# A two-branch merge whose second addend arrives by accumulating DMAs begun on GpSimd

## The chip, the core and the metric

The kernel runs on one core of one Trainium2 chip. The time is what the device took for one execution, in microseconds, and the median of several runs is compared. The profile is of one further execution, so sums made from it are made against its own time.

The names of the engines in the profile are PE (TensorE, the matmuls), PEld (its weight loads), DVE (VectorE), ACT (ScalarE), POOL (GpSimd) and SP (SyncE, which here only begins DMAs). A "q" behind a name is the engine's instruction queue.

## The reference

One step of a decoder layer, in float32, over 1024 prompt rows and 64 sample rows with 1024 channels. The change touches only the merge of its two branches.

```python
h = rmsnorm(x, norm_mix)
q, k, v, gu, gv, ga, gb = split_in(h @ w_in)
o = attention(q, k, v)                        # sliding window of 128, sinks
s = spatial_gating(gelu(gu), layernorm(gelu(gv)))
merged = sigmoid(ga) * (o @ w_pa) + sigmoid(gb) * (s @ w_pb)
x = x + merged @ w_out
x = x + conv_ffn(rmsnorm(x, norm_ffn))        # up, causal conv, gelu gate, down
y = rmsnorm(x, norm_final)
```

## The kernel before, in words

Everything is kept transposed: 128 channels on the partitions, rows along the free dimension. The 1024 channels are eight column blocks, numbered c = 0 to 7. The 1088 rows are cut in two groups: group 0 has 576 rows (the 64 sample rows and half the prompt), group 1 has 512. Each float32 operand of a matmul is split into a high and a low part (ACT casts the high one, DVE subtracts to get the low one), and three matmuls stand for one product; this pair of steps is the helper `split`, lines 40 and 41. For weights the tiles are called wraw, wh and wl, for the merged operand mh and ml.

The stages around the change, in order of time:

- Attention of group 0, mixed with the gMLP branch product (`branch`). For each c and both groups, DVE multiplies the product in PSUM by the gate (line 1072), and SP stores the result to memory, in `mbd[g][c]`.
- Attention of group 1, mixed with the attention branch product of group 0 (`merge(0, c, keep)`). For each c DVE multiplies by the other gate (line 1100, tile stg, 576 wide), and `keep` stores the result to memory, in `msd[c]`.
- The merge of group 1 (`merge(1, c, ...)`): 48 matmuls for each c, then DVE multiplies by the gate (line 1100, 512 wide), adds the gMLP half, which SP had loaded from `mbd[1][c]` into a second staging tile (line 1102), and splits the sum. Beside it, for each c, `hold` loads `msd[c]` and `mbd[0][c]` of group 0 into the tiles m and b, DVE adds them (line 1403), and `operand(0)` splits the sum.
- w_out, first of group 0 and then of group 1 (line 240 again, and the residual add on line 1419), and after it the up projection.

During the last two stages ACT and DVE also prepare the first up-projection weights (`pair_load`, `pair_unit`; tiles ra, rb, s and hl), which are stored to `upd`.

Names that the prediction uses: stg is the staging tile, of which there are four (gates, products and, before, the second addend); mm is the accumulator in PSUM, of which there are two; sg0d is the gate in memory; mask c is the causal mask that POOL applies in attention (line 1277), and s the scores, into which POOL copies a sink column (line 1240).

The program order is written in Python; a scheduler then lays out each engine's instructions in a fixed order, and each engine runs its own in that order and waits on semaphores. A DMA is an instruction in the queue of the engine that begins it, and what stands behind it waits while it waits.

Of the kernel before, what the change touches and what calls it, by code (L numbers as in the profile page):

```python
# [6 lines left out]
F32 = mybir.dt.float32  # L7
# [3 lines left out]
ALU = mybir.AluOpType  # L11
# [4 lines left out]
P = 128  # L16
D = 1024
KD = 8
# [16 lines left out]
def layer(tc, a):  # L35
    nc = tc.nc
    V, S, G, PE = nc.vector, nc.scalar, nc.gpsimd, nc.tensor

    def split(hi, lo, src):
        S.copy(hi, src)  # L40
        V.tensor_sub(lo, src, hi.bitcast(F32))  # L41
# [5 lines left out]
    with ExitStack() as top:  # L47
# [185 lines left out]
        def mm3(ps, chunks, w, hs, k0, k1, nk, clear=True):  # L233

            wh, wl = w
            for lo, c0, c1 in chunks:
                for k in range(k0, k1):
                    ah, al = hs[k]
                    for i, (u, v) in enumerate(((wh, ah), (wh, al), (wl, ah))):
                        PE.matmul(ps[:, lo:lo + c1 - c0], u[:, k, :], v[:, c0:c1],  # L240
                                  start=(clear and k == 0 and i == 0),
                                  stop=(k == nk - 1 and i == 2), skip_group_check=True)
# [91 lines left out]
        dr = lambda name, shape, dt=F32: dram.tile(shape, dt, name=name)  # L334
# [9 lines left out]
        gvd = {name: dr(f"gvd{name}", [P, GW]) for gr in groups for name, _ in gr["toks"]}  # L344
        vnd = [dr(f"vnd{gr['g']}", [P, NG, len(gr["toks"]), P]) for gr in groups]
        sd_ = [[dr(f"sd{g}{c}", [P, 2, n]) for c in range(NG)] for g, n in ((0, 576), (1, 512))]
        msd = [dr(f"msd{c}", [P, 576]) for c in range(KD)]
        upd = [[dr(f"upd{f}_{j}", [P, 2, 4, P]) for j in range(7)] for f in range(NPRE)]
        mbd = [[dr(f"mbd{g}{c}", [P, n]) for c in range(KD)] for g, n in ((0, 576), (1, 512))]

# [7 lines left out]
        with ExitStack() as ph1:  # L358
# [9 lines left out]
            def stage(n):  # L368
                return stg.tile([P, 576], F32, name="stg")[:, :n]
# [346 lines left out]
            none = lambda: None  # L716
# [319 lines left out]
            def acc2():  # L1036
                return pmm.tile([P, 1024], F32, name="mm")
# [41 lines left out]
            def gate(g, c):  # L1079
                n, off = groups[g]["n"], groups[g]["off"]  # L1080
                t = stage(n)
                nc.sync.dma_start(t, sgd[0][c][:, off:off + n])
                return t

            def merge(g, c, to, early=False):

                st, n, off, base = {}, *(groups[g][x] for x in ("n", "off", "base"))

                def part(e, k0):
                    def go():  # L1090
                        if e == k0 == 0:
                            st["t"] = first_gate.pop() if first_gate else gate(g, c)
                            if g:
                                st["u"] = stage(n)
                                nc.sync.dma_start(st["u"], mbd[g][c])
                            st["w"], st["ps"] = W.get(), acc2()
                        mm3(st["ps"], groups[g]["chunks"][e:e + 1], st["w"], os_[g], k0, k0 + 4, KD,
                            e == 0 or not early)
                        if e and k0:
                            V.tensor_mul(st["t"], st["t"], st["ps"][:, base:base + n])  # L1100
                            if g:
                                V.tensor_add(st["t"], st["t"], st["u"])
                            to(c, st["t"])
                    return go
                order = [(e, k0) for e in range(2) for k0 in (0, 4)]
                return [part(*x) for x in (sorted(order, key=lambda x: x[1]) if early else order)]
# [227 lines left out]
            first_gate.append(gate(0, 0))  # L1334
            for go in prepare(groups[1]):
                go()
            keep = lambda c, t: nc.sync.dma_start(msd[c], t)
            ms, own1 = [[], []], []
            over = [x for c in range(KD) for x in merge(0, c, keep)]
            first = merge(1, 0, lambda c, t: own1[0](c, t), True)  # L1340
# [8 lines left out]
            def operand(g):  # L1349
                def go(c, t):  # L1350
                    hl = tuple(hmp[g].tile([P, groups[g]["n"]], F32R, name=f"m{x}{c}") for x in "hl")
                    split(*hl, t)
                    ms[g].append(hl)
                return go

            pwo, pair = ExitStack(), {}
            pwp = pwo.enter_context(tc.tile_pool(name="pw", bufs=1, reuse_waits="tile"))

            def pair_load(f):
                def go():  # L1360
                    store()
                    for e, name in enumerate("ab"):
                        pair[name] = pwp.tile([P, KD, P], F32, name=f"r{name}")
                        nc.sync.dma_start(pair[name], wt(UP0 + f + NFF * e))
                return go

            def pair_unit(f, j):

                def go():
                    store()  # L1370
                    ta, tb = pair["a"], pair["b"]
                    a11, a12, a21, a22 = ta[:, 0:4], ta[:, 4:8], tb[:, 0:4], tb[:, 4:8]
                    src = {0: a11, 5: a12, 6: a22}.get(j)
                    if src is None:
                        x, y = ((a21, a22), (pair.get("s1"), a11), (pair.get("s2"), a12), (a11, a21))[j - 1]
                        src = pair[f"s{j}"] = pwp.tile([P, 4, P], F32, name="s", bufs=2)
                        V.tensor_add(src, x, y)
                    t = pwp.tile([P, 2, 4, P], F32R, name="hl", bufs=2)
                    split(t[:, 0], t[:, 1], src)
                    pair["store"] = upd[f][j], t.bitcast(F32)  # L1380
                return go
# [5 lines left out]
            held = {}  # L1387

            def hold(c):
                if c < KD:  # L1390
                    held[c] = [pwp.tile([P, 576], F32, name=x, bufs=3) for x in "mb"]
                    for x, src in zip(held[c], (msd[c], mbd[0][c])):
                        nc.sync.dma_start(x, src)

            hold(0)
            hold(1)
            ahead = [x for f in range(NPRE) for x in (pair_load(f), *(pair_unit(f, j) for j in range(7)))]
            own1.append(operand(1))
            for c in range(KD):
                for at, go in enumerate(merge(1, c, operand(1)) if c else [none, none, *first[2:]]):  # L1400
                    if at == 1:
                        t, u = held.pop(c)
                        V.tensor_add(t, t, u)
                        operand(0)(c, t)
                        hold(c + 2)
                    go()
                    if at == 2 and c % 2:
                        ahead.pop(0)()
            bo[1].close()

            def x_of(gr, c):
# [253 lines left out]
        later, held = [], {}  # L1665
# [335 lines left out]
```

## Time and profile before

| | before |
|---|---|
| median of 3 runs | 1514.14 us (1513.75 to 1515.58) |
| the profiled execution, its own time | 1515.38 us |
| its span in the trace | 1513.6 us |
| PE busy in the span | 1496.9 us, 99% |
| DVE, ACT, POOL busy | 1158.1, 825.9, 265.8 us |
| granted TensorE clock, mean | 0.997 |
| attention of group 1 | about 580 to 680 us |
| merge of group 1 | about 680 to 714 us |
| w_out of group 0 begins | 713.93 us |

In the profile's rows, "out<-in" names the tiles, x is a count, and a bracket holds the idle time before an instruction and what ended it. A row of the chain of waits has a start, a length and what took that time. A row of waits has who waited, for whom, the total in us, how often, and the longest. Busy times by stretch have, for each engine, the busy us and in brackets the number of instructions.

### The profile page before, as it was taken

What the parts mean: (1) busy time and instruction counts of PE and PEld (TensorE: products, weight loads), DVE (VectorE), ACT (ScalarE), POOL (GpSimd) and SP (SyncE); (2) the same over time, 40 slices, a digit from 0 to 9 for tenths busy, and PEclk for the clock granted to TensorE, in tenths of its full rate; (3) what the DMA queues carried; (4) which work ended last, traced back from release to release, by engine and by line L of the source; (5) the groups of instructions that cost most, each with busy time, mean ns of one, the idle gap of its engine ahead of it and who ended that gap; (6) DMA issues with size and microseconds to landing.
All of it is one profiled execution on the core that took longest, in us unless ns stands there. A gap on an engine that the chain in (4) does not pass through costs nothing.

```text
span 1513.6 us, 31400 instructions
## 1 busy us (share of the span) xinstructions
PE 1496.9 (99%) x12190; PEld 1482.8 (98%) x12190; DVE 1158.1 (77%) x1909; ACT 825.9 (55%) x1755; POOL 265.8 (18%) x422
## 2 busy tenths in 40 slices
PE   9999999999999999999999999999999999999997
PEld 9999999999999999999999999999999999999997
DVE  6896777756645895989668888898898888785685
ACT  6665764554543774864444555555555556453463
POOL 0000012200120222430222221332142122000002
PEclk9999999999999999999999999999999999999998
DMA  8453457737749758749988323332243226983363
GB/s 289 156 188 111 178 175 269 224 127 269 242 172 324 251 188 224 233 169 303 335 281 282 129 107 123 110 127 108 90 143 109 87 79 217 359 267 97 117 189 131
DMA packets 137508, 286.70 MB, mean 189 GB/s; under 512 B 15248, under 2 KB 44368, under 8 KB 137360
## 3 DMA queue, kind: packets, MB, share of 16 engines
q1 hardware_dynamic: 132352, 279.97, 55.2%
q10 hardware_dynamic: 5008, 4.73, 0.9%
q8 instruction: 96, 1.57, 0.4%
q14 instruction: 52, 0.43, 0.1%
HBM read 195.76 MB, written 90.85 MB: 189 GB/s over the span
## 4 chain that ended last, share of the span: by engine, by line
PE 76%; DVE 4%; ACT 2%; issue 1%; DMA 1%; POOL 0%; SPq 0%; DVEq 0%; ACTq 0%; POOLq 0%
PE st L300 41%; PE dn L1740 15%; PE mm L240 14%; PE sc L1233 1%; PE pt L1266 1%; PE mx L841 1%; ACT s L1256 1%; DVE wl L41 1%; DMA q<-qd 1%; PE po L1294 1%; DVE s L1259 0%; DVE nm L1249 0%; DVE v L767 0%; PE po L1297 0%; DVE s L1243 0%
## 5 line engine op out<-in xcount | busy, mean ns | idle before, releaser
L300 PE MATMUL st<-th,wh 128*128 128x256 f32 (+1 forms) x2128 | 610.7, 287 | 1.8 <-ACT ku L283 1.3
L300 PE MATMUL st<-tl,wh 128*128 128x256 f32 (+1 forms) x2128 | 608.6, 286 | 0.0
L300 PE MATMUL st<-th,wl 128*128 128x256 f32 (+1 forms) x2128 | 608.2, 286 | 0.0
L300 PEld LDWEIGHTS st<-th,wh 128*128 128x128 f32 x2128 | 400.0, 188 | 3.7 <-ACT k L281 1.7
L300 PEld LDWEIGHTS st<-th,wl 128*128 128x128 f32 x2128 | 400.2, 188 | 0.0
L300 PEld LDWEIGHTS st<-tl,wh 128*128 128x128 f32 x2128 | 399.8, 188 | 0.0
L40 ACT CAST wh<-wraw 128x512 fp32r<-128x512 f32 (+2 forms) x204 | 139.5, 694 | 92.6 <-PE st L300 35.3
L41 DVE TENSOR_TENSOR wl<-wraw,wh 128x512 fp32r<-128x512 f32 (+2 forms) x204 | 159.3, 793 | 36.8 <-ACT wh L40 34.8
L1740 PE MATMUL dn<-th,wh 128*128 128x288 f32 (+1 forms) x616 | 176.8, 287 | 0.0
L1740 PE MATMUL dn<-tl,wh 128*128 128x288 f32 (+1 forms) x616 | 176.2, 286 | 0.0
L1740 PE MATMUL dn<-th,wl 128*128 128x288 f32 (+1 forms) x616 | 175.1, 284 | 0.0
L40 ACT CAST wh<-ws 128x512 fp32r<-128x512 f32 x160 | 98.1, 622 | 101.0 <-PE st L300 64.1
L41 DVE TENSOR_TENSOR wl<-ws,wh 128x512 fp32r<-128x512 f32 x160 | 109.2, 695 | 47.4 <-ACT wh L40 45.5
L1740 PEld LDWEIGHTS dn<-th,wl 128*128 128x128 f32 x616 | 115.9, 188 | 0.0
L1740 PEld LDWEIGHTS dn<-th,wh 128*128 128x128 f32 x616 | 115.6, 188 | 0.1
L1740 PEld LDWEIGHTS dn<-tl,wh 128*128 128x128 f32 x616 | 115.7, 188 | 0.0
L288 POOL TENSOR_TENSOR z<-ku,k 128x256 f32<-128x256 f32 (+1 forms) x32 | 29.3, 918 | 316.6 <-ACT ku L283 315.3
L41 DVE TENSOR_TENSOR tl<-traw,th 128x544 fp32r<-128x544 f32 (+1 forms) x85 | 61.3, 729 | 21.1 <-ACT th L40 21.1
L40 ACT CAST th<-traw 128x544 fp32r<-128x544 f32 (+1 forms) x85 | 53.8, 642 | 43.2 <-PE dn L1740 27.1
L240 PE MATMUL mm<-s,wh 128*128 128x256 f32 (+1 forms) x384 | 76.6, 293 | 0.0
L531 PE MATMUL st<-w2h,th 128*128 128x256 f32 x308 | 74.5, 283 | 0.3 <-DVE w2l L165 0.3
L240 PE MATMUL mm<-ol,wh 128*128 128x256 f32 (+1 forms) x256 | 73.5, 288 | 0.4 <-DVE ol L41 0.4
(300 smaller groups left out, 3161.5 us busy)
## 6 DMA issues: line engine op xcount, KB each, us to landing
wraw<-wt SPq DMA_DIRECT2D x133, 512.0 KB
traw<-td SPq DMA_DIRECT2D x77, 272.0 KB
td<-za SPq DMA_DIRECT2D x22, 544.0 KB
wraw<-wt SPq DMA_DIRECT2D x35, 256.0 KB
upd<-hl SPq DMA_DIRECT2D x14, 512.0 KB
td<-t SPq DMA_DIRECT2D x11, 544.0 KB
qd<-q SPq DMA_DIRECT2D x8, 576.0 KB
q<-qd SPq DMA_DIRECT2D x8, 576.0 KB
```

Source lines behind the costliest of these rows:

```text
L40: S.copy(hi, src)
L41: V.tensor_sub(lo, src, hi.bitcast(F32))
L240: PE.matmul(ps[:, lo:lo + c1 - c0], u[:, k, :], v[:, c0:c1], start=(clear and k == 0 and i == 0), stop=(k == nk - 1 and i == 2), skip_grou ...
L288: op(to, pick(x, to, lo, hi), pick(y, to, lo, hi))
L300: PE.matmul(ps, u[:, kk, :], v, start=first and kk + i == 0, stop=kk == 3 and i == 2, skip_group_check=True)
L531: PE.matmul(ps, u, v[:, k, :], start=k + i == 0, stop=k == KD - 1 and i == 2)
L841: PE.matmul(ps[:, P * i:P * i + P], vn[:, i], late["wst"][:, c, :], start=True, stop=True)
L1233: PE.matmul(ps[:, h, o0:256], q, kst[kv][:, e, k0:cur + P], start=e == 0, stop=e == 1)
L1256: S.activation(s[:, h], s[:, h], AF.Exp, bias=nm[:, h:h + 1], accum_out=dn[:, h:h + 1])
L1266: PE.transpose(pt[:, h * P:h * P + P], s[:, h, 0:P], ident)
L1294: PE.matmul(half(po, e), v[:, b - 1 + e], half(x, e), start=e == 0 and x is ph, stop=False, skip_group_check=True)
L1740: PE.matmul(place(m, e), u[:, m, :], v[:, lo:hi], start=new and i + k == 0 and (e == 0 or m % 2 == 0), stop=i == NU - 1 and k == 2, skip_g ...
```

## The change

Both additions of the two branches leave DVE. For group 0, `keep` begins a DMA on GpSimd that adds the tile to `mbd[0][c]` in memory, where the other half already stands; `msd` goes, and `hold` loads one tile instead of two. For group 1, a DMA begun on GpSimd adds `mbd[1][c]` from memory into the staging tile; the second staging tile goes. The split of group 1's block c is written one block later, in the last part of block c + 1.

```diff
-        msd = [dr(f"msd{c}", [P, 576]) for c in range(KD)]
...
                             st["t"] = first_gate.pop() if first_gate else gate(g, c)
-                            if g:
-                                st["u"] = stage(n)
-                                nc.sync.dma_start(st["u"], mbd[g][c])
                             st["w"], st["ps"] = W.get(), acc2()
...
                             V.tensor_mul(st["t"], st["t"], st["ps"][:, base:base + n])
                             if g:
-                                V.tensor_add(st["t"], st["t"], st["u"])
+                                G.dma_start(st["t"], mbd[g][c], accum_op=ALU.add)
                             to(c, st["t"])
...
-            keep = lambda c, t: nc.sync.dma_start(msd[c], t)
+            keep = lambda c, t: G.dma_start(mbd[0][c], t, accum_op=ALU.add)
...
                 if c < KD:
-                    held[c] = [pwp.tile([P, 576], F32, name=x, bufs=3) for x in "mb"]
-                    for x, src in zip(held[c], (msd[c], mbd[0][c])):
-                        nc.sync.dma_start(x, src)
+                    held[c] = pwp.tile([P, 576], F32, name="m", bufs=3)
+                    nc.sync.dma_start(held[c], mbd[0][c])
...
-            own1.append(operand(1))
+            own1.append(lambda c, t: summed.append((c, t)))
+            summed = []
             for c in range(KD):
-                for at, go in enumerate(merge(1, c, operand(1)) if c else [none, none, *first[2:]]):
+                for at, go in enumerate(merge(1, c, own1[0]) if c else [none, none, *first[2:]]):
                     if at == 1:
-                        t, u = held.pop(c)
-                        V.tensor_add(t, t, u)
-                        operand(0)(c, t)
+                        operand(0)(c, held.pop(c))
                         hold(c + 2)
+                    if at == 3 and summed:
+                        operand(1)(*summed.pop(0))
                     go()
                     if at == 2 and c % 2:
                         ahead.pop(0)()
+            operand(1)(*summed.pop(0))
```

PE's order of instructions stays as it was. Three places of the other engines' orders matter to the prediction. In all rows, "waits DMASW" is a wait for a DMA that GpSimd began, "DMAHW" for one that SP or ACT began. The numbers in the tile names differ between the two programs and only tell tiles apart.

DVE in the merge of group 1, around the multiply by the gate of block 3 (`stg<-stg,mm`); before:

```order
L1100 TENSOR_TENSOR stg_9436<-stg_9436,mm_9446 128x512 [waits DMAHW6_49,PE_49]
L41 TENSOR_TENSOR ml3_9535<-m_9386,mh3_9534 128x576 [waits Activation_49,Pool_49]
L1102 TENSOR_TENSOR stg_9436<-stg_9436,stg_9438 128x512 [waits DMAHW7_49,DVE_49]
L41 TENSOR_TENSOR wl_9594<-wraw_9440,wh_9593 128x1024
L41 TENSOR_TENSOR ml2_9507<-stg_9436,mh2_9506 128x512 [waits Activation_49]
L1100 TENSOR_TENSOR stg_9510<-stg_9510,mm_9520 128x512 [waits DMAHW2_49,PE_49]
```

The first row is the multiply of block 2, the last that of block 3. The same place now:

```order
L1096 TENSOR_TENSOR stg_9410<-stg_9410,mm_9418 128x512 [waits DMASW6_49,PE_49]
L41 TENSOR_TENSOR ml1_9462<-stg_9337,mh1_9461 128x512 [waits DMASW1_49,Activation_49]
L41 TENSOR_TENSOR ml4_9573<-m_9435,mh4_9572 128x576 [waits DMAHW2_49]
L41 TENSOR_TENSOR wl_9625<-wraw_9481,wh_9624 128x1024 [waits DMAHW0_49,Activation_49]
L41 TENSOR_TENSOR ml5_9642<-m_9504,mh5_9641 128x576 [waits DMAHW4_49,DVE_49,Activation_49]
L1373 TENSOR_TENSOR s_9672<-rb_9390 128x512 [waits DMAHW0_49]
L41 TENSOR_TENSOR ml2_9534<-stg_9410,mh2_9533 128x512 [waits DMASW2_49,Activation_49]
L41 TENSOR_TENSOR ml6_9717<-m_9576,mh6_9716 128x576 [waits DMAHW6_49]
L41 TENSOR_TENSOR hl_9674<-s_9672,hl_9674 128x512 [waits Activation_49]
L1096 TENSOR_TENSOR stg_9479<-stg_9479,mm_9487 128x512 [waits DMAHW3_49,DMASW7_49,PE_49]
```

The add is gone, and the split of block 2 (`ml2<-stg`), which waits for the accumulate of block 2, stands between the multiplies of block 2 and of block 3. The later blocks look alike: the split of block k stands between the multiplies of blocks k and k + 1.

ACT at the start of the merge, the casts of the first two blocks; before:

```order
L40 CAST wh_9593<-wraw_9440 128x1024 [waits DMAHW5_49,PE_49]
L40 CAST mh0_9354<-stg_9236 128x512 [waits DVE_49]
L40 CAST mh1_9382<-m_9315 128x576 [waits DVE_49]
L40 CAST mh1_9432<-stg_9358 128x512 [waits DVE_49]
L40 CAST hl_9566<-ra_9414 128x512 [waits DMAHW7_49,DMAHW3_49]
```

And now:

```order
L40 CAST hl_9530<-ra_9388 128x512 [waits DMAHW7_49,DMAHW3_49,DMAHW1_49]
L40 CAST mh0_9392<-stg_9228 128x512 [waits DMASW0_49]
L40 CAST mh3_9500<-m_9362 128x576 [waits DMAHW1_49,Pool_49]
L40 CAST mh4_9572<-m_9435 128x576 [waits DMAHW2_49,Pool_49]
L40 CAST mh1_9461<-stg_9337 128x512 [waits DMASW1_49]
L40 CAST wh_9624<-wraw_9481 128x1024 [waits DMAHW0_49,PE_49]
```

The casts of group 1 wait for a DMA where they waited for DVE, and those of group 0 (`m`) stand further ahead.

POOL in attention of group 1, at group 0's block 3 (masks `c`, sink column `s`); before:

```order
L1277 AFFINE_SELECT c_8409<-ph_8405 64x4x64 [waits Activation_49]
L1277 AFFINE_SELECT c_8409<-ph_8405 64x4x64 [waits Pool_49]
L1277 AFFINE_SELECT c_8409<-pl_8406 64x4x64 [waits DVE_49]
L1277 AFFINE_SELECT c_8409<-pl_8406 64x4x64
L1240 COPY s_8593<-c_sinkb_475 128x4 [waits DVE_49,PE_49,Pool_49]
```

And now:

```order
L1273 AFFINE_SELECT c_8401<-ph_8397 64x4x64 [waits Activation_49]
L1273 AFFINE_SELECT c_8401<-ph_8397 64x4x64 [waits Pool_49]
L1273 AFFINE_SELECT c_8401<-pl_8398 64x4x64 [waits DVE_49]
L1273 AFFINE_SELECT c_8401<-pl_8398 64x4x64
L1333 DMA mbd03_190<-stg_8330 128x576 [waits DVE_49]
L1236 COPY s_8585<-c_sinkb_467 128x4 [waits DVE_49,PE_49,Pool_49]
```

The accumulate stands between the masks and the next sink copy, and waits for DVE's multiply. Sixteen such DMAs are in POOL's queue in all: eight here, and eight in a row in the merge, where POOL has nothing else to do.

## The prediction

> **What bounds the kernel now.** I read the page's busy times first, then busy times by stretch around the edited lines, then TensorE's (PE's) waits there, then the chain that ended last, and only then single rows.
>
> ```profile
> span 1513.6 us, 31400 instructions
> PE 1496.9 (99%) x12190; PEld 1482.8 (98%) x12190; DVE 1158.1 (77%) x1909; ACT 825.9 (55%) x1755; POOL 265.8 (18%) x422
> ...
> 580.00:593.00 13.00, 12.45 (x95) 12.25 (x94) 4.05 (x6) 1.59 (x3) 0.95 (x1) 1.00 0.95 262
> 593.00:665.00 72.00, 71.70 (x555) 69.24 (x556) 65.06 (x120) 56.68 (x177) 28.67 (x68) 1.00 0.72 218
> 665.00:680.00 15.00, 13.55 (x107) 12.43 (x106) 11.01 (x23) 7.87 (x24) 4.29 (x10) 1.00 0.55 191
> 680.00:722.00 42.00, 42.00 (x361) 42.00 (x361) 39.98 (x57) 20.99 (x29) 0.00 (x0) 1.00 0.88 298
> ...
> PE pt L1266 <- DVE s L1259: 1.8, 5, 0.8
> PE sc L1233 <- DMA q<-qd: 0.5, 1, 0.5
> PE mm L240 <- DVE ol L41: 0.4, 1, 0.4
> ...
> 678.67 91.85 PE mm L240 x742
> ```
>
> PE is busy 99% of the span. The stretches are attention of group 1 (580 to 680) and the merge of group 1 with the start of w_out (680 to 722); their columns are length, busy PE, weight loads, DVE, ACT, POOL, clock, DMA share, GB/s. PE's idle time sums to 2.3 us from 580 to 680, from small waits on softmax, the q load and the operand split, none of them an edited line. From 678.67 the chain is 91.85 us of matmuls without a break, though VectorE (DVE) is busy 39.98 of 42.00 us. So the adds that go stand beside PE work, and the question is whether the new transfers make PE wait.
>
> **Where the merge has slack.** A column block c of the merge is 48 matmuls.
>
> ```profile
> 684.00:712.00 28.00, 28.00 (x249) 28.00 (x248) 1.00 0.93 319
> ...
> 713.93 0.30 PE L240 MATMUL mm<-mh,wh 128*128 128x320 f32 x1
> ...
> 720.28 0.31 PE L240 MATMUL mm<-mh,wh 128*128 128x320 f32 x1
> ...
> 680.02 0.69 DVE L1100 TENSOR_TENSOR stg<-stg,mm 128x512 f32<-128x512 f32 x1 [0.94 <-PE mm L240]
> ...
> 689.45 0.68 DVE L41 TENSOR_TENSOR hl<-ra,hl 128x512 fp32r<-128x512 f32 x1
> 690.05 0.68 DVE L1100 TENSOR_TENSOR stg<-stg,mm 128x512 f32<-128x512 f32 x1
> 690.65 0.75 DVE L41 TENSOR_TENSOR ml<-m,mh 128x576 fp32r<-128x576 f32 x1
> 691.32 0.68 DVE L1102 TENSOR_TENSOR stg<-stg 128x512 f32<-128x512 f32 x1
> 691.92 1.22 DVE L41 TENSOR_TENSOR wl<-wraw,wh 128x1024 fp32r<-128x1024 f32 x1
> 693.05 0.68 DVE L41 TENSOR_TENSOR ml<-stg,mh 128x512 fp32r<-128x512 f32 x1
> ...
> 682.94 0.61 ACT L40 CAST mh<-stg 128x512 fp32r<-128x512 f32 x1
> ...
> 672.97 0.59 ACT L40 CAST ph<-pt 128x512 fp32r<-128x512 f32 x1 [1.20 <-PE pt L1266]
> ...
> 673.66 0.69 DVE L41 TENSOR_TENSOR pl<-pt,ph 128x512 fp32r<-128x512 f32 x1 [0.80 <-ACT ph L40]
> ```
>
> 249 matmuls in 28.00 us, two of them reaching over an edge, are 0.1133 us each, so a block takes 5.44 us. The first 320-wide matmul is w_out's block 0, at 713.93; block 1 begins at 720.28, so one takes 6.35. Counting back, merge blocks 2 to 7 begin at 681.29, 686.73, 692.17, 697.61, 703.05 and 708.49. There are two accumulators, so the multiply by the gate (L1100; mul k below) must end before block k+2 begins: mul 5 by 708.49, mul 6 by 713.93, mul 7 by 720.28, w_out's first residual add by 726.63. The starts of DVE's rows show what each occupies: 0.60 at 512 elements, 0.67 at 576, 1.13 at 1024. From ACT's cast to DVE's subtraction 0.10 us pass (673.56 to 673.66).
>
> **The change, part by part.**
>
> Removed adds: eight of L1102 at 0.60 and eight of L1403 at 0.67, 10.2 us of DVE. PE waited for nothing there (42.00 of 42.00), so they are worth 0. The 24 SP issues that go (8 stores to msd, 8 loads of b, 8 of stg<-mbd) are worth 0 likewise: the loads were consumed by those adds, and PE's weights were on time.
>
> Group 1's accumulate into the tile. The split of block k now waits for memory, not for DVE, and the order shows it in DVE's queue ahead of a later mul. Let L be the time from the end of mul k to the landing. After landing come ACT's cast 0.61, DVE's subtraction 0.60 and some 0.24 of hand-offs: 1.45. Following DVE's new order, mul 0 ends at 680.65 as before, its split at 682.10 + L; an hl, a wl, an ml and mul 2 (0.60 + 1.13 + 0.67 + 0.60) end mul 2 at 685.10 + L. From there each mul waits for the split of the block before it:
> mul 3 ends at 685.10 + L + (L + 1.45 + 0.65 + 0.60 + 0.60) = 688.40 + 2L;
> mul 4, 5, 6 each L + 1.45 + 0.60 + 0.60 later: mul 5 at 693.70 + 4L, mul 6 at 696.35 + 5L;
> mul 7 L + 2.05 later, 698.40 + 6L; the residual add L + 4.25 later (split, two sums and an hl, the add), 702.65 + 7L.
> Against the limits the delay of PE is the largest of 4L − 14.8, 5L − 17.6, 6L − 21.9, 7L − 24.0, and nothing below L = 3.4. From 678.67 to 770 PE never pauses, so a delay goes to the end.
>
> L is in no row of before; nearest are these.
>
> ```profile
> 579.61 2.00 DMA mbd<-stg
> 583.92 8.89 DMA q<-qd
> ...
> 713.63 0.33 SPq L331 DMA_DIRECT2D stg<-xt  x1
> 714.01 0.43 SPq L1385 DMA_DIRECT2D upd<-hl  x1
> ...
> 719.29 0.62 ACT L40 CAST hl<-s 128x512 fp32r<-128x512 f32 x1 [2.36 <-DMA upd<-hl]
> ```
>
> Low end: a plain 256 KB store of the same tile shape lands in 2.00 us. High end: a 512 KB store in the merge itself, 714.01 to 719.29, 5.28 us. An accumulate takes in 512 KB (tile and memory) and writes 256 KB, with the DMA engines at 0.88 to 0.93, so it is nearest the second; that one stood behind a 288 KB load issued 0.38 us earlier, 0.9 us at 319 GB/s, which leaves 4.4. I take L = 4.35: 7 × 4.35 − 24.0 = 6.5 us. At the ends, 0 and 13.0.
> The Trainium skill, "DMA: Bandwidth & Descriptors", section "Anatomy of one DMA — SWDGE (gpsimd) path", fits a GpSimd DMA at about 2.0 us plus its bytes at 436 GB/s. By that estimate 256 KB take 2.6 us and PE would not wait; no run here shows it, and it is for a plain copy on free engines.
>
> Group 0's accumulate into memory. In attention, POOL now holds the DMA between its masks.
>
> ```profile
> 619.16 0.74 DVE L1100 TENSOR_TENSOR stg<-stg,mm 128x576 f32<-128x576 f32 x1
> ...
> 619.31 0.89 POOL L1277 TENSOR_SCALAR_AFFINE_SELECT c<-pl 64x256 fp32r<-64x256 f32 x2 [0.24 <-DVE pl L41]
> 623.17 0.19 POOL L1240 COPY s<-c_sinkb 128x4 f32<-128x4 f32 x1 [2.97 <-PE pt L1266]
> ...
> L1337 SPq DMA_DIRECT2D msd<-stg x8: 319/326/547, 589.2 to 665.3; - x8
> ...
> 786.43 1.29 POOL L1429 TENSOR_TENSOR nacc<-nacc,stg 128x512 f32<-128x512 f32 x1 [5.96 <-ACT stg L1428]
> ```
>
> The wait for the mul costs POOL nothing here: the mul ends at 619.90, POOL's masks at 620.20, and the next POOL step waits until 623.17. To begin the DMA takes POOL between 0.3 us (SP's issue) and, say, 1.3 (an ordinary POOL step at 512 elements); I take 1, hidden in the 2.97 idle. Price 0; behind it stand only the sink copies and masks, whose users are DVE and PE. SP's staging loads (sg0d) now wait for a landed accumulate; behind them in SP's queue are weight loads with four buffers, price 0. The first accumulate starts near 587, beside the q load for which PE waits at 592.86 already; between 0 and 1.1 us (288 KB more read at 262 GB/s), I take 0.5.
>
> **Sum.** 6.5 + 0.5 = 7.0 us. The profiled execution took 1515.4 us with a span of 1513.6; the median of the runs is 1514.1. So the span goes to 1520.6 and the median to 1521.1.
>
> **Rivals.** (a) The accumulates land early, L up to 3.4: no PE wait, 1514 us, at best 0.5 better. For it: 2.00 us above, fewer bytes once b is gone, and a queue of its own that need not stand behind SP's. Against it: the engines are 0.93 busy and memory is read as well. It decides at 3.4; at 3.8 the loss is 2.6 plus 0.5. The skill's fit is on this side.
> (b) POOL becomes late in attention: if beginning a DMA costs over 3 us instead of 1, masks or sink copies come late, perhaps 1 us at each of five blocks, 1519 us without the merge wait. For it: in-order masks behind the DMA. Against it: idle gaps like 2.97.
> (c) DVE relief counts after all, since DVE is 95% busy in the merge: faster by at most the 2.3 us of idle PE from 580 to 680, 1512. Against it: the removed adds all run later than that.
> (d) That no accumulate happens is excluded: the order has sixteen DMAs on POOL.
>
> **How the numbers follow.** The merge wait 0.58, (a) 0.28, (b) 0.10, (c) 0.04. A change under 0.2%, 3 us, can't be told from none. Of the first case some 0.06 falls under 3 us, so slower 0.63, same 0.32, faster 0.05 with (c) and a little for the unforeseen. The range runs from 1513.5, where (a) ends, to 1528.5, where L = 5.28 and the full q delay give 13.0 + 1.1; within the first case alone it is 1516 to 1528.5.
>
> **What would show it.** Right: PE waits of 1 to 2 us in the merge at "PE mm L240 <- DVE stg" of the gate multiply or at the residual add, ACT's mh<-stg ended by the accumulate DMA, 4 to 5 us from mul to landing, DVE with idle time there. Wrong: PE 42 of 42 busy in the merge with landings under 3.4 us (a), or new PE waits on POOL's c or on s in attention (b). A landing that takes much more than 5.3 us would carry the loss beyond the range.

## The result: 1540.0 us, slower by 1.7%

The median of five runs is 1540.02 us, against 1514.14 before; the ratio is 1.0173 (95% interval 1.0160 to 1.0186), or 26.2 us (24.2 to 28.2). One of the five runs of the kernel before took 2098.77 us and is left out of the ratio. The forecast had the right sign and the right place, a wait of the multiplies for the landing of group 1's accumulates, but its size was 7 us, with 14 as its upper end.

The page of the profile after, the busy times by stretch, and PE's waits:

```profile
span 1536.4 us, 31394 instructions
PE 1502.8 (98%) x12190; PEld 1488.4 (97%) x12190; DVE 1147.3 (75%) x1893; ACT 825.0 (54%) x1755; POOL 272.7 (18%) x438
...
593.00:665.00 72.00, 71.69 (x559) 69.25 (x558) 66.27 (x124) 56.87 (x180) 34.09 (x75) 1.00 0.80 211
...
680.00:722.00 42.00, 33.04 (x256) 32.53 (x255) 22.46 (x32) 13.10 (x20) 4.40 (x5) 0.88 0.83 234
722.00:745.00 23.00, 16.97 (x116) 16.42 (x115) 6.06 (x8) 4.69 (x7) 1.75 (x2) 0.93 0.75 222
...
PE mm L240 <- ACT hl L40: 9.8, 3, 6.0
PE mm L240 <- DVE stg L1096: 8.8, 3, 4.8
```

Attention (593 to 665) is as it was, 71.69 of 72.00 us. From 680 to 722 PE was busy 42.00 us before and is busy 33.04 now, and DVE, which lost sixteen adds, fell from 39.98 to 22.46: it stands still. PE has six new waits in two rows, 18.6 us in sum. The row that names ACT's hl, a cast for the up projection, is of the same kind: in all six PE began again 0.14 to 0.15 us after the end of DVE's multiply or residual add (716.91 after 716.76, 748.66 after 748.51), and the hl cast only happened to end beside it. PE's idle time in the span grew by 16.9 us (33.6 less 16.7), and its busy time by 5.9, because the granted clock fell to 0.88 and 0.93 here (and to 0.89 from 745 to 775).

Who waits for what is read in ACT's and DVE's waits from 677 to 750, the DMA queues and issues from 676 to 745 (packets, MB and share of 16 engines; the last number of an issue is the median from begin to landing), and a piece of the chain that ended last:

```profile
ACT mh L40 <- DMA stg<-mbd: 43.4, 8, 8.4
...
DVE ml L41 <- ACT mh L40: 29.1, 8, 6.9
...
q0 software_dynamic: 1152, 2.10, 18.8%
stg<-mbd POOLq DMA_DIRECT2D x8, 256.0 KB, 6.9
...
717.38 6.60 DMA stg<-mbd
723.98 0.02 issue
724.00 0.63 ACT mh L40
724.63 0.02 issue
724.66 0.04 DVE ml L41
...
725.27 0.69 DVE hl L41
725.95 0.60 DVE stg L1096
...
736.54 7.92 DMA stg<-mbd
744.46 0.02 issue
744.48 0.63 ACT mh L40
...
748.66 45.32 PE mm L240 x336
```

This is the loop of the prediction: an accumulate begins (717.38) and lands 6.60 us later, ACT casts, DVE subtracts, and only then DVE reaches the next multiply (725.95), whose accumulate can then begin. Between 726.55 and 736.54 the chain, by another hl cast, goes over a load of ra; the rows there show that the multiply of block 7 came behind a landing too, that of the accumulate begun at 727.17:

```profile
733.98 0.62 ACT L40 CAST mh<-stg 128x512 fp32r<-128x512 f32 x1 [7.89 <-DMA stg<-mbd]
...
734.63 0.69 DVE L41 TENSOR_TENSOR ml<-stg,mh 128x512 fp32r<-128x512 f32 x1 [6.95 <-ACT mh L40]
735.24 0.68 DVE L1096 TENSOR_TENSOR stg<-stg,mm 128x512 f32<-128x512 f32 x1
```

From 748.66 PE runs without a break. Every step is where it was forecast; the length of the landing is not.

### The profile page after: what moved, and what is told of

Same layout as the page of the kernel before. It is cut to its first block, busy times and chain, and to the rows that moved or that the text cites. A ratio compares the mean times of both kernels' runs of the same rounds, so it can differ in the third digit from the quotient of the medians.

```text
span 1536.4 us, 31394 instructions
## 1 busy us (share of the span) xinstructions
PE 1502.8 (98%) x12190; PEld 1488.4 (97%) x12190; DVE 1147.3 (75%) x1893; ACT 825.0 (54%) x1755; POOL 272.7 (18%) x438
## 4 chain that ended last, share of the span: by engine, by line
PE 50%; DMA 1%; DVE 1%; ACT 1%; issue 0%; DVEq 0%; SPq 0%; ACTq 0%
PE st L300 29%; PE dn L1737 15%; PE mm L240 5%; DMA stg<-mbd 1%; DMA ra<-wt 0%; ACT c L1618 0%; PE fs L1772 0%; DVE wl L41 0%; PE fs L1788 0%; ACT wh L40 0%; PE st L1550 0%; PE sc L1472 0%; DVE c L1620 0%; DVE c L1619 0%; DVE s L1373 0%
## 5 line engine op out<-in xcount | busy, mean ns | idle before, releaser
L240 PE MATMUL mm<-mh,wh 128*128 128x256 f32 (+1 forms) x256 | 74.8, 292 | 9.7 <-ACT hl L40 7.3
L240 PE MATMUL mm<-oh,wh 128*128 128x256 f32 (+1 forms) x256 | 75.4, 296 | 9.0 <-DVE stg L1096 6.4
L41 DVE TENSOR_TENSOR tl<-traw,th 128x544 fp32r<-128x544 f32 (+1 forms) x85 | 61.5, 730 | 24.2 <-ACT th L40 24.0
```

What stands on the lines that cost most here:

```text
L240: PE.matmul(ps[:, lo:lo + c1 - c0], u[:, k, :], v[:, c0:c1], start=(clear and k == 0 and i == 0), stop=(k == nk - 1 and i == 2), skip_grou ...
```

## What each half does, and what the later split does

All ratios below are to the kernel before, run beside the kernel named; a ratio is put into us by 1514.

**Group 0's half alone.**

```diff
-keep = lambda c, t: nc.sync.dma_start(msd[c], t)
+keep = lambda c, t: G.dma_start(mbd[0][c], t, accum_op=ALU.add)
```

> Only group 0's half of the change: its eight accumulates into memory stay, the merge of group 1 is as before (SP load, DVE add). Theory (the loss is the landing of group 1's accumulates, which stands in DVE's and ACT's queues ahead of the next multiply): no PE wait in the merge, 1514 us, within 2 us. Rival (group 0's accumulates, 4 to 10 us each from begin to landing, hold up staging tiles or masks and carry part of the loss): 1518 us or more. The PE work stood 3.1 us earlier at the start of the merge in the changed kernel's profile; if that comes from group 0's half, this kernel should be 1511 to 1512.

1514.80 us, ratio 1.0004 (0.9994 to 1.0014), no new PE wait. Group 0's half costs nothing and brings nothing, though it takes eight adds from DVE. In this trace PE stood 1.6 us earlier than before at the end of attention, but that means nothing: in the profiles of all kernels here that place lies between 0.2 us later and 3.4 us earlier, and 3.0 earlier with the later split alone (next but one), which changes nothing ahead of the merge.

**Group 1's half alone.** The rest of the diff, with msd, its loads and DVE's adds for group 0 left in.

> Only group 1's half: its accumulates into the tile with the split one block later; group 0's half is stored, loaded and added as before. Theory (landing chain of group 1): the whole loss, 1540 us, up to 1546 since the 288 KB load of b for each block comes back and shares the DMA engines with the accumulate, landings of 7.5 to 8.5 us. Rival (group 0 carries part of it): under 1532.

1537.43 us, ratio 1.0160 (1.0139 to 1.0181), 24 us: the whole loss within the intervals. The median landing was 6.7 us, and no longer for the extra loads, so that part of the expectation missed.

**The later split without an accumulate.** SP loads and DVE adds as before; only the split of group 1 is written a block later.

> No accumulate: loads and adds as before for both groups, but the split of group 1 written one block later, as in the changed kernel. Theory: the later split alone costs nothing, since nothing in it waits for memory: 1514, within 2 us. Rival (the later split holds staging tiles longer, and the loads behind them come late): 1518 or more.

1514.30 us, ratio 1.0000 (0.9991 to 1.0009). The later split is free by itself.

**GpSimd's loads ahead of the multiply.**

```diff
-nc.sync.dma_start(st["u"], mbd[g][c])
+G.dma_start(st["u"], mbd[g][c])
```

> The kernel before, with the loads of group 1's second addend begun by GpSimd instead of SP, before the block's matmuls as there; DVE adds. Theory (a slow landing costs only where it starts after the multiply): landings of 4 to 8 us, hidden under the block, 1514 within 2 us. Rival (GpSimd's transfers slow SP's beside them): 1518 or more.

1514.88 us, ratio 0.9999 (0.9990 to 1.0009), with a median landing of 6.0 us. Transfers nearly as slow as those of the change (6.9 us) cost nothing where they begin a block ahead of their use, nor do they harm SP's beside them.

## What makes the landing long

Four kernels have the same steps and differ in the transfer of the 256 KB: the changed kernel, and three that load the 256 KB plainly into the same tile after the multiply, so that the same steps wait for it.

```diff
 V.tensor_mul(st["t"], st["t"], st["ps"][:, base:base + n])
 if g:
-    G.dma_start(st["t"], mbd[g][c], accum_op=ALU.add)
+    G.dma_start(st["t"], mbd[g][c])        # or nc.sync, or nc.scalar
```

> The changed kernel with group 1's accumulate replaced by a plain GpSimd load of the same 256 KB into the same tile at the same place (the sum is left out: group 1 keeps the gMLP half alone). Theory S (the landing is long because a GpSimd transfer starts 1.6 to 2.8 us after its begin and its packets then share the engines with 1.6 MB of other transfers): landings stay at 6 to 7 us, 1530 to 1540. Rival A (reading, adding and writing makes the transfer slow): landings of 3 to 4 us, 1514 to 1520.

> As the plain GpSimd load, but begun by SP (the sum is left out here too). Theory S: the start is 1 to 2 us earlier but it stands behind SP's other transfers, landings of 5 to 6 us, 1522 to 1532, and SP itself waits for each multiply with weight loads behind. Rival B (GpSimd's queue is what is slow): landings of 2 to 3.5 us, under 1518.

> As the plain load, but begun by ACT, a hardware queue other than SP's (the sum is left out). SP's plain load reached ACT's cast 2.6 to 5.7 us after its multiply, GpSimd's landed 3.9 to 8.9 after. Theory Q (what is slow is GpSimd's start, 1.3 to 3 us to the first packet): ACT's load lands like SP's, 3 to 5 us, 1516 to 1522. Rival (a second queue shares every engine packet by packet with SP's later transfers, while on SP's own queue those stand behind): landings of 5 to 7, 1526 or more.

L is the time from the end of a multiply to the landing (for SP and ACT, to the start of ACT's cast, which can be later). The prediction's largest term is 7L − 24.0 and holds seven landings, those of blocks 0 and 2 to 7. The delay in the trace is the growth of the time from attention's last matmul to the up projection's first.

| transfer begun by | mean of the seven L | 7L − 24.0 | delay in the trace | ratio (interval), in us |
|---|---|---|---|---|
| SP, plain | 4.23 | 5.6 | 4.2 | 1.0040 (1.0025 to 1.0055), 6.1 |
| ACT, plain | 5.43 | 14.0 | 14.5 | 1.0091 (1.0077 to 1.0105), 13.8 |
| GpSimd, plain | 6.40 | 20.8 | 22.0 | 1.0146 (1.0129 to 1.0163), 22.1 |
| GpSimd, accumulating | 7.09 | 25.6 | 26.6 | 1.0173 (1.0160 to 1.0186), 26.2 |

The term holds over the whole range, to 1.5 us. One pair of rows for its ends: with SP, DVE's multiply (L1096) and ACT's cast behind the transfer; with GpSimd's accumulate the same pair.

```profile
707.44 0.68 DVE L1096 TENSOR_TENSOR stg<-stg,mm 128x512 f32<-128x512 f32 x1
...
710.72 0.62 ACT L40 CAST mh<-stg 128x512 fp32r<-128x512 f32 x1 [0.77 <-DMA stg<-mbd]
```

```profile
716.08 0.68 DVE L1096 TENSOR_TENSOR stg<-stg,mm 128x512 f32<-128x512 f32 x1
...
717.38 0.87 POOL L1098 DMA_DIRECT2D stg<-mbd  x1 [9.26 <-ACT hl L40]
...
724.00 0.62 ACT L40 CAST mh<-stg 128x512 fp32r<-128x512 f32 x1 [7.18 <-DMA stg<-mbd]
```

2.60 us, the shortest of SP's, against 7.24. Three of the kernels have the transfer on a queue of its own, so that L can be cut in parts. Counted by packets (not a view of the profile), the means of the same seven are:

| transfer begun by | multiply to begin | begin to first packet | first to last packet | to landing (ACT: to cast) |
|---|---|---|---|---|
| ACT, plain | 0.03 | 1.96 | 2.96 | 0.48 |
| GpSimd, plain | 0.51 | 1.92 | 3.48 | 0.50 |
| GpSimd, accumulating | 0.53 | 2.36 | 3.76 | 0.44 |

The three steps of L are 1.2, 1.0 and 0.7 us:

- From SP's queue to ACT's. SP waits for the multiply with its other transfers behind it, so what SP begins later stands behind the load; on any other queue the load meets it in the engines. This reading is argued from the order of the queues. I had expected ACT's load to land like SP's; the expectation's rival came true, and SP's own landings lie between its two. The order of ACT's own instructions differs too, so the step is not sharing alone.
- From ACT's queue to GpSimd's: half of the step is that the plain load begins 0.4 to 0.6 us after the multiply instead of at once, the other half lies between the first packet and the last. GpSimd's first packets come 1.3 to 3.0 us after the begin, but ACT's come 1.0 to 2.8 after theirs, so a slow start of GpSimd's is not the cause of this step.
- From the plain load to the accumulate: 0.4 us before the first packet and 0.3 behind it. This step is not clear of noise: the intervals of the two ratios overlap, and single landings differ by more. The accumulate does take more engine time. The queues from 676 to 745, for the plain load:

```profile
q0 software_dynamic: 640, 2.10, 11.0%
stg<-mbd POOLq DMA_DIRECT2D x8, 256.0 KB, 6.1
```

The accumulate moves the same 2.10 MB in 1152 packets and 18.8% of the engines, the plain load in 640 and 11.0%: 1.62 against 0.95 us of 16 engines for each transfer (share × 69 us / 8). Neither is near 6 us, and of the 0.67 us more only 0.3 show between first and last packet. During the landing that began at 717.38, the two queues were:

```profile
q1 hardware_dynamic: 467, 1.59, 65.4%
q0 software_dynamic: 144, 0.26, 32.8%
```

SP's queue moved 1.59 MB beside the 0.26 MB of the accumulate. Counted by packets, from 720.50 to 722.50 the accumulate held 7.8 of the 16 engines in the mean and SP's queue 8.2, in packets of 2 KB against 4 KB, whose medians were 176 and 173 ns. The Trainium skill, "DMA: Bandwidth & Descriptors", section "Queues, rings and completion order", says that each engine goes round its queues packet by packet; those two us agree. By the fit in the Trainium skill, "DMA: Bandwidth & Descriptors", section "Anatomy of one DMA — SWDGE (gpsimd) path", which is given per DMA (that it is for a plain copy on free engines is the prediction's own reading), a GpSimd transfer of 256 KB takes an estimated 2.6 us; none here did, the nearest being 3.6 us for a plain one (issue at 678.27).

**Less traffic beside it.** The preparation of the up projection (loads of ra and rb, stores to upd) goes behind w_out's first residual add.

```diff
-                    if at == 2 and c % 2:
-                        ahead.pop(0)()
...
-                for _ in range(1 + c % 2):
-                    ahead.pop(0)()
                 x1_tile(groups[0], c, ps, xt)
+                with tc.issue_after(pair["x1"]):        # the store of x1_tile
+                    for _ in range(2):
+                        ahead.pop(0)()
```

> The changed kernel with all up-projection preparation (loads of ra and rb, stores to upd) moved behind w_out's first residual add, so that some 0.5 MB of other transfers per block are gone from the merge. Theory S: landings of 4.5 to 5.5 us, PE's waits between the multiplies of the merge fall from 18.7 to under 8 us; the time of the whole is not a fair comparison, since w_out has the work instead. Rival A (the accumulate is slow in itself): landings stay near 7, waits of 15 us or more.

```profile
stg<-mbd POOLq DMA_DIRECT2D x8, 256.0 KB, 5.7
...
PE mm L240 <- DVE stg L1096: 10.3, 6, 2.9
```

The bytes moved beside one of the last four accumulates fell from 1.6 to 1.8 MB to about 0.8, the median landing from 6.9 to 5.7 us, and PE's waits for the multiplies from 18.6 to 10.3. Both are a little above what was expected: in these last four the packets took 2.0 to 3.2 us instead of 3.6 to 4.8 from first to last, but the first came 3.1 to 3.4 us after the begin, against 1.6 to 2.8. Why it came later with less traffic stays open. The whole took 1539.20 us, ratio 1.0182 (1.0164 to 1.0200), no faster than the changed kernel: in the trace the time from w_out's first matmul to the up projection's is 12.5 us longer than before.

## Taking the wait off the way

**The split one block further back.** The split of block k goes behind the multiply of block k + 1, and is held there on ACT and DVE.

```diff
-                    if at == 3 and summed:
-                        operand(1)(*summed.pop(0))
                     go()
+                    if at == 3 and len(summed) > 1:
+                        operand(1)(*summed.pop(0))
```

> The changed kernel, with the split of group 1's block k placed behind the multiply of block k + 1 on DVE and ACT (of the last block behind w_out's first residual add). A landing then has 5.4 us more. Theory (the wait stands ahead of the multiply): one loop now spans two blocks, 7.4 + 3 against 10.9 us, so PE's waits in the merge fall from 18.7 to under 3 us and the time is 1514 to 1518, the granted clock does not drop there. Rival (the transfers themselves crowd the DMA engines and make weights late): waits of over 10 us stay, 1530 or more.

1525.76 us, ratio 1.0077 (1.0063 to 1.0090), 11.7 us: more than half of the loss is gone, but the expectation missed, and PE's waits were 8.1 us where under 3 was expected. The rows of ACT and DVE ahead of the multiply of block 6:

```profile
718.16 0.62 ACT L40 CAST mh<-stg 128x512 fp32r<-128x512 f32 x1 [3.96 <-DMA stg<-mbd]
718.68 0.61 ACT L40 CAST hl<-rb 128x512 fp32r<-128x512 f32 x1
...
719.33 0.69 DVE L41 TENSOR_TENSOR hl<-rb,hl 128x512 fp32r<-128x512 f32 x1 [4.41 <-ACT hl L40]
719.93 0.68 DVE L1096 TENSOR_TENSOR stg<-stg,mm 128x512 f32<-128x512 f32 x1
```

DVE no longer waits for the split there. But ACT waits for the landing in its own queue (718.16), a cast of the up projection's preparation stands behind that (718.68), and DVE needs that cast before the multiply. This wait of PE's, 4.7 of the 8.1 us, had moved to ACT's queue.

**Two blocks further back** (`len(summed) > 2`, the last two behind w_out's first residual adds).

> As the later split, by one more block: the split of block k stands behind the multiply of block k + 2, on ACT too. With one block, ACT's cast of block 5 still waited for its landing (718.13) ahead of a cast that DVE needs before the multiply of block 6, and PE lost 4.7 us there. Theory (only the place of the wait matters): landings stay at 5 to 9 us but nothing on the way to a multiply waits for them, PE's waits in the merge under 2 us, 1513 to 1517. Rival (GpSimd's transfers crowd out weights, stores and staging tiles): over 1520.

1523.14 us, ratio 1.0055 (1.0043 to 1.0068): 8.3 us left, above the expectation and in the range of its rival. PE's waits and DVE's:

```profile
PE mm L240 <- DVE stg L1096: 5.7, 3, 2.2
...
DVE hl L41 <- ACT hl L40: 16.0, 7, 5.6
```

DVE waits 16.0 us for casts of the preparation (10.7 in the kernel before, where PE waited for no multiply). Two of PE's three waits, 2.1 and 2.2 us, came the same way, over a cast that stands on ACT behind the wait for a landing. The third, 1.5 us, did not: there ACT's cast (726.21) waited 6.3 us for a load of ra, begun by SP at 715.78, which took 10.3 us. So one transfer was late here in the rival's sense.

**Two blocks, and the preparation moved** as in the quieter kernel above.

> The split two blocks later, and besides all up-projection preparation moved behind w_out's first residual add, so that ACT's casts for it no longer stand between the casts of group 1's blocks (in the kernel before this one DVE waited 16.0 us for such casts, which stood on ACT behind the wait for a landing, and PE 5.7 us for the multiplies behind those). Theory (what is left of the loss comes over ACT's queue): PE's waits between the multiplies of the merge under 0.5 us, though landings stay at 5 to 8 us; the whole is still 4 to 6 us above the kernel before, since w_out then carries the preparation (waits of about 4 us there in the kernel with early splits). Rival (transfers crowd out weights): PE waits of 3 us or more stay in the merge.

```profile
PE mm L240 <- DVE x1g L1413: 2.5, 1, 2.5
PE mm L240 <- DVE stg L1096: 1.4, 1, 1.4
```

1521.66 us, ratio 1.0044 (1.0027 to 1.0061). In the merge one wait of 1.4 us is left of 18.6, where under 0.5 was expected, with landings still at 6.0 us in the median. So landings of this length don't make PE wait by themselves; the place of the wait does, on DVE's queue and on ACT's. The preparation's own loads and stores are gone from the merge as well, so this kernel doesn't tell its casts from the load of ra that came late above. w_out now pays for the preparation: from its first matmul on it adds 5.0 of the 7.3 us by which the first up-projection matmul comes later. No version was faster than the kernel before.

## Why the prediction was right and wrong

- **The chain of waits: right.** The split's place in DVE's queue, the largest term 7L − 24.0 and the way to the end of the kernel came out. With the measured L and PE 3.15 us earlier than in the profile before, mul 7 should end at 736.4 and w_out's first residual add at 749.1; they ended at 735.9 and 748.5.
- **The step that failed: L.** The term 7L − 24.0 was mis-sized. L was taken as 4.35, "nearest the second" row, a 512 KB store in SP's queue, with 5.28 as the upper bound. It measured 7.09: 0.53 us from the multiply to the begin on POOL, 2.36 to the first packet, 3.76 from the first packet to the last beside SP's traffic, and 0.44 to the landing. The value 4.35 fits SP's queue, where a plain load has 4.23; that it fits is luck, since it was made for an accumulate. A plain load begun by ACT already had 5.43, so the bounds, both from SP's queue, were no bounds for another one. With seven landings in the chain, 2.74 us too few make 19.2 us, which is the miss. What sets the time to the first packet stays open.
- **Removed adds and issues at 0: right** for group 0's, by the kernel with that half alone. Group 1's eight adds were not taken out by themselves.
- **Beginning a DMA on POOL at 1 us: right** in size (0.87 to 1.07 us for group 0) and hidden; rival (b) had no case.
- **The q load, 0.5 us: not seen.** PE's gap near 592 is 0.55 us before and absent in the changed kernel; in the seven kernels that have the same group 0 half and differ from the changed one only after it, it is 0 (two of them) or 0.3 to 0.8. It varies by itself.
- **Rival (a), landings up to 3.4: fell.** No accumulate in any kernel here landed in less than 3.9 us from its begin, even at 652.24 in the changed one (4.1), where the engines were nearly idle.
- **Left out: the clock.** The prediction had PE's delay equal the wait. PE's waits also lowered the granted clock (below). The chain set the pace meanwhile, so it adds only where PE restarts at 748.66 with half the clock until 751.87, 1.6 us.

## What to carry to other kernels

A landing is priced on the queue that begins it, at the traffic of its place, and multiplied by how often a chain goes through it. Before an add is put into a transfer, look at what stands behind the wait on every engine that uses the result: an add of 0.6 us was replaced by a wait of 7, and the wait came back over ACT when it was taken from DVE. A transfer that begins a block ahead may be slow; one that begins behind the step that makes its operand may not.

## What the runs showed of the hardware

- The accumulate of 256 KB into the tile used 144 packets (128 of 2 KB, and small ones) where GpSimd's plain load used 80, and one of its 2 KB packets took 176 ns, about as long as one of 4 KB (159 to 173); the plain load begun by ACT used packets of 2 KB too, and one of them took 84 ns. All packets together, one accumulate took 1.62 us of all engines, GpSimd's plain load 0.95.
- With the engines at 0.19 beside it, GpSimd's accumulate of 288 KB into memory still took 4.1 us from begin to landing (652.24 to 656.32), 1.4 of them until the first packet.
- PE's waits lower the granted clock afterwards. The busy times from 690 to 720 of the changed kernel:

```profile
690.00:700.00 10.00, 8.33 (x73) 8.16 (x73) 9.38 (x14) 4.93 (x8) 0.89 (x1) 1.00 0.94 275
700.00:710.00 10.00, 5.22 (x33) 5.06 (x32) 3.93 (x6) 2.08 (x3) 0.88 (x1) 0.70 0.63 172
710.00:720.00 10.00, 7.49 (x53) 7.32 (x53) 3.63 (x5) 2.60 (x4) 0.87 (x1) 0.84 0.75 202
```

  The wait of 1.7 us in the first stretch left it at 1.00; in the one of 4.8 us in the second, 2.1 us after it began, the clock went to half for 6.8 us (704.09 to 710.92). In the merges and w_outs of all kernels here every wait of 2.4 us or more (rounded) brought 3.4 or 6.8 us at half the clock, a single one under 1.9 never, and between the two some (once also two of 1.7 and 0.4 us close together).
